# Moving a kernel's main SBUF pool down by 128 bytes: weight buffers and operand tiles at another distance

## The chip, the cores and the metric

The kernel runs on one core of a Trainium2 chip. TensorE (PE) multiplies matrices into PSUM; VectorE (DVE) and ScalarE (ACT) do elementwise work; GpSimd (POOL) and SyncE (SP) here mostly issue DMAs. The metric is the device time of one execution in microseconds (us). Before the change three runs took 2003.82, 2023.43 and 2035.96 us; the median is 2023.43 us.

SBUF addresses in this document are byte addresses within a partition, as the built program has them. All 128 partitions use the same address for a tile.

## The reference, cut to what matters

One decoder layer on 512 tokens of width 2048, all in float32:

```python
mod = (c_act @ w_ada[l] + b_ada[l]).reshape(B, N_MOD, D)        # 2048 x 12288
h = rmsnorm(x, g_norm_mix[l]) * (1.0 + sc1) + sh1
proj = jnp.einsum('bsd,de->bse', h, w_in[l])                    # 2048 x 5120
o_attn = stick_breaking_attention(...)                          # 8 heads of 128
hr = rg_lru(causal_depthwise_conv(xr, ...), ...)                # width 1024
mixed = concat([rmsnorm(o_attn, ...), rmsnorm(hr * gelu(xg), ...)])
x = x + gt1 * einsum('bse,ed->bsd', mixed, w_out[l])            # 2048 x 2048
h = rmsnorm(x, g_norm_mlp[l]) * (1.0 + sc2) + sh2
hid = square(relu(einsum('bsd,df->bsf', h, w_mlp_in[l])))       # 2048 x 8192
x = x + gt2 * einsum('bsf,fd->bsd', hid, w_mlp_out[l])          # 8192 x 2048
return rmsnorm(x, g_norm_final)
```

## The kernel before, in words

**Matmuls.** Each float32 factor is split into a rounded high part and the low remainder, and every product is three matmuls: high by high, high by low, low by high (`mm3`, L258; the same three written out at L470 to L472 and at L1099 to L1101). A matmul has a stationary operand of 128 columns, brought in by its own weight load (PEld in the profile), and a moving operand that streams past it. While one matmul streams, the weight load of the next one runs.

**Stages.** Up to about 660 us the projections of `w_in`, the attention heads, the recurrence and the first three quarters of `w_out` are worked out, mostly with moving operands of 512 columns. From there on the moving operands are 256 columns wide (half of the tokens): the last quarter of `w_out` and the first block of the MLP (`half_product`, L988), then the other 15 blocks of the MLP's first matrix and its second matrix by a Strassen-like scheme with seven products in place of eight (`strassen`, L1080). Each step of that scheme loads one block of 1024 weight columns, forms four sums of its quarters on DVE (L1057, L1064, L1065), splits quarters and sums into high and low parts (`operands`, L1050), and issues 7 products x 2 halves x 3 = 42 matmuls. The last stretch is a normal product and the output.

**Buffers.** Moving operands of the MLP are `a` tiles, 64 buffers of 2,048 bytes. Three quarters of a weight block, split, lie in `w3` buffers (3,072 bytes, called small here); the four sums, split, lie in buffers of 4,096 bytes (called large), which `T` takes in turn from the tags `w4` four times and `w5` once (L82, L98). Of the seven products of a step, the four with t1 to t4 read large buffers and the other three read `w3` (`PRODUCTS`, L1075).

**Where they lie.** The main pool `sp` begins low in SBUF with constants, then `ga` (16 bytes a buffer, laid out at a pitch of 32), then `pad` (L140, `PAD` floats that nothing uses), then `cb`, `n` and `a`. On top of it, on the left side, stands one of two pools that follow each other in time: `front` (`wr`, `wh`, `wl`) and `mlp`, which begins with `shift` (`SHIFT` = 16 floats that nothing uses), then `w5` and `w3`. The right side hangs from the top of SBUF and doesn't depend on the main pool: `x` and `tt` first, later `ts`, `raw` and `w4`. In the built program before the change:

| tiles | address of the first | remainder by 512 |
|---|---|---|
| `cb`, `n`, `a` | 19,904, 28,096, 38,336 | 448 |
| `wr`, `wh`, `wl` | 169,408, 177,600, 183,744 | 448 |
| `w5`, `w3` | 169,472, 173,568 | 0 |
| `x`, `tt`, `ts`, `raw`, `w4` | 192,000, 208,384, 192,000, 200,192, 212,480 | 0 |

Every buffer of a tag has the same remainder, and every slice that a matmul takes of one begins a multiple of 512 bytes into it. So a weight load of the MLP begins 64 bytes behind the moving operand, modulo 512, for large and small buffers alike; with `wh` and `a` in the earlier stages the distance is 0.

**What sets the order.** A scheduler orders each engine's instructions by data dependence and by priorities that the kernel gives (`tc.high_priority`). `ga` holds the partial sums of a DVE operation (L211, L1200) until a second DVE operation adds them up (L220, L1206).

Of the kernel before, what the change touches and what calls it, by code (L numbers as in the profile page):

```python
# [40 lines left out]

URGENT = 150
EVAC = 88
PAD, SHIFT = 24, 16

BUFS = {"cb": 2, "a": 64, "ga": 4, "n": 5}
COLS = {
    "wr": 512, "wh": 512, "wl": 512, "x": 1024, "cb": 1024, "tt": 1280, "n": 512, "a": 512, "ga": 4,  # L50
    "raw": 1024, "ts": 1024, "w3": 768, "w4": 1024, "w5": 1024, "shift": SHIFT,
# [13 lines left out]
def hybrid_layer_kernel(  # L65
# [35 lines left out]
    def new(tag, dt=F32, cols=None):  # L101
        count[0] += 1
        pool, bufs = (sp, BUFS[tag]) if tag in BUFS else pools[tag][:2]
        return pool.tile([P, cols or COLS[tag]], dt, tag=tag, name=f"{tag}_{count[0]}", bufs=bufs)
# [1355 lines left out]
```

## Time and profile before

| what | value |
|---|---|
| runs before | 2003.82, 2023.43, 2035.96 us |
| the profiled execution's own time | 2022.22 us |
| its span, first to last instruction | 2020.5 us |
| mean granted TensorE clock | 0.995 |
| matmuls | 14,532 |
| PE busy | 1967.8 us (97%) |
| DVE busy | 1761.0 us (87%) |
| ACT busy | 1076.0 us (53%) |

The views give busy time of an engine, the number of instructions (x), and the mean duration of one. Matmuls overlap, so their durations add up to more than the time; how often one starts is read from a count in a stretch of time. An instruction counts in a stretch if any part of it lies there, so a stretch in which matmuls of duration d follow each other without a gap holds (stretch + d) / (time from start to start) of them.

### The profile page before, as it was taken

To read this page: it belongs to the slowest core of one execution; us is meant where nothing else is said; L and a number is where in the kernel's file an instruction comes from. 1 tells how busy PE (TensorE), PEld (TensorE's weight loads), DVE (VectorE), ACT (ScalarE), POOL (GpSimd) and SP (SyncE) were. 2 spreads that over 40 slices of the span, in tenths; PEclk is the share of its full clock that TensorE was granted. 3 is DMA by queue.
4 is the path that set the end of the run, shared out by engine and by line. 5 is a ranking of instruction groups with operands and counts; after the bars stand their busy time and mean duration, and the time that the engine had idled before them with its cause. 6 is when DMAs were issued, how large, how long until landed. Compare 5 with 4: busy or idle time off the path is not lost. (4 is left out here: it accounts for less than half of the span.)

```text
span 2020.5 us, 37927 instructions
## 1 busy us (share of the span) xinstructions
PE 1967.8 (97%) x14532; PEld 1857.3 (92%) x14532; DVE 1761.0 (87%) x2971; ACT 1076.0 (53%) x1572; POOL 181.1 (9%) x283
## 2 busy tenths in 40 slices
PE   8999999999999998999999999999999999999997
PEld 6789898788888998999999999999999999999996
DVE  8998776878998599999999999999778778778986
ACT  5443564786433385555555555456445555555542
POOL 0000000000000000112112112200011110210000
PEclk9999999999999999999999999999999999999998
DMA  9896655546779544666666657665486667667744
GB/s 363 301 319 211 211 158 179 182 151 217 229 251 360 171 137 150 216 202 218 204 196 228 209 178 230 222 205 179 142 300 224 222 243 250 234 243 256 241 152 152
DMA packets 205624, 441.45 MB, mean 218 GB/s; under 512 B 20353, under 2 KB 41985, under 8 KB 205442
## 3 DMA queue, kind: packets, MB, share of 16 engines
q1 hardware_dynamic: 178642, 360.78, 54.1%
q0 software_dynamic: 21760, 71.32, 9.5%
q10 hardware_dynamic: 5040, 6.93, 1.0%
q8 instruction: 114, 1.87, 0.4%
q14 instruction: 68, 0.56, 0.1%
HBM read 375.25 MB, written 63.70 MB: 217 GB/s over the span
## 5 line engine op out<-in xcount | busy, mean ns | idle before, releaser
L1101 PE MATMUL ps_mm<-a,w 128*128 128x256 f32 x1696 | 472.4, 279 | 1.6 <-DVE w L122 1.6
L1099 PE MATMUL ps_mm<-a,w 128*128 128x256 f32 x1696 | 472.0, 279 | 1.9 <-DVE a L1111 1.1
L1100 PE MATMUL ps_mm<-a,w 128*128 128x256 f32 x1696 | 472.3, 279 | 0.2 <-DVE a L122 0.2
L1069 ACT ACTIVATE w<-ts 128x1024 fp32r<-128x1024 f32 x244 | 258.4, 1059 | 249.4 <-DVE ts L1065 224.8
L1101 PE MATMUL ps_z<-a,w 128*128 128x256 f32 x1304 | 364.8, 280 | 7.5 <-DVE w L122 7.5
L1099 PE MATMUL ps_z<-a,w 128*128 128x256 f32 x1304 | 364.6, 280 | 3.1 <-ACT a L1110 1.5
L122 DVE TENSOR_TENSOR w<-ts,w 128x1024 fp32r<-128x1024 f32 x244 | 297.5, 1219 | 79.0 <-PE ps_mm L1100 44.6
L1100 PE MATMUL ps_z<-a,w 128*128 128x256 f32 x1304 | 364.0, 279 | 0.1
L1099 PEld LDWEIGHTS ps_mm<-a,w 128*128 128x128 f32 x1696 | 321.5, 190 | 2.5 <-issue 2.0
L1101 PEld LDWEIGHTS ps_mm<-a,w 128*128 128x128 f32 x1696 | 318.8, 188 | 2.1 <-DVE w L122 2.0
L1100 PEld LDWEIGHTS ps_mm<-a,w 128*128 128x128 f32 x1696 | 318.6, 188 | 0.6 <-DVE a L122 0.6
L1063 ACT ACTIVATE w<-raw 128x768 fp32r<-128x768 f32 x244 | 204.6, 839 | 211.9 <-PE ps_mm L1100 101.0
L122 DVE TENSOR_TENSOR w<-raw,w 128x768 fp32r<-128x768 f32 (+1 forms) x296 | 267.0, 903 | 35.7 <-ACT w L244 22.7
L1101 PEld LDWEIGHTS ps_z<-a,w 128*128 128x128 f32 x1304 | 246.0, 189 | 9.2 <-DVE w L122 9.1
L1099 PEld LDWEIGHTS ps_z<-a,w 128*128 128x128 f32 x1304 | 248.0, 190 | 4.5 <-ACT a L1110 1.7
L1100 PEld LDWEIGHTS ps_z<-a,w 128*128 128x128 f32 x1304 | 245.7, 188 | 0.6 <-DVE a L122 0.6
L244 ACT ACTIVATE wh<-wr 128x512 fp32r<-128x512 f32 (+1 forms) x184 | 113.1, 618 | 150.9 <-PE ps_mm L262 67.6
L259 PE MATMUL ps_mm<-a,wh 128*128 128x512 f32 x448 | 176.5, 394 | 4.0 <-DVE a L460 1.7
L263 PE MATMUL ps_mm<-a,wl 128*128 128x512 f32 x448 | 175.5, 392 | 1.0 <-DVE wl L122 0.7
L1057 DVE TENSOR_TENSOR ts<-raw 128x512 f32<-128x512 f32 x244 | 166.4, 683 | 10.2 <-DMA raw<-in_w_mlp_out_dram 9.7
L262 PE MATMUL ps_mm<-a,wh 128*128 128x512 f32 x448 | 174.7, 390 | 0.0
L211 DVE SCALAR_TENSOR_TENSOR x<-x,cb 128x1024 f32<-128x1024 f32 x108 | 131.1, 1217 | 29.5 <-DMA x<-in_w_adaT_dram 29.3
(332 smaller groups left out, 4137.9 us busy)
## 6 DMA issues: line engine op xcount, KB each, us to landing
raw<-in_w_mlp_out_dram SPq DMA_DIRECT2D x124, 512.0 KB, 4.1
raw<-in_w_mlp_in_dram SPq DMA_DIRECT2D x120, 512.0 KB, 3.8
x<-in_w_adaT_dram SPq DMA_DIRECT2D x108, 512.0 KB, 5.9
wr<-in_w_in_dram SPq DMA_DIRECT2D x160, 256.0 KB, 3.5
tt<-in_w_adaT_dram SPq DMA_DIRECT2D x52, 512.0 KB, 6.8
part<-a POOLq DMA_DIRECT2D x84, 256.0 KB, 3.8
a<-part SPq DMA_DIRECT2D x84, 256.0 KB, 6.4
prod<-a POOLq DMA_DIRECT2D x63, 256.0 KB, 5.9
```

What stands on the lines that cost most here:

```text
L122: tt(out=out, in0=full, in1=f32(high), op=ALU.subtract)
L211: ins = stt(out=t, in0=t, scalar=1.0, in1=cb[q_], op0=ALU.mult, op1=ALU.mult, accum_out=self.ga[:, q_ : q_ + 1],)
L244: act(h[:, :n], r[:, :n], AF.Copy)
L259: first = mm(out, wh, ah, start=start, stop=False, **kw)
L262: mm(out, wh, al, start=False, stop=False, **kw)
L263: mm(out, wl, ah, start=False, stop=stop, **kw)
L1057: tt(out=t[:, : 2 * HT].rearrange("p (a b) -> p a b", a=2), in0=r[:, HT : 3 * HT].rearrange("p (a b) -> p a b", a=2), in1=r[:, q_(0)].unsq ...
L1063: act(h, r[:, HT:], AF.Copy)
L1069: act(h, t, AF.Copy)
L1099: mm(out, wh[:, blk(i)], ah, start=st, stop=False, **kw)
L1100: mm(out, wh[:, blk(i)], al, start=False, stop=False, **kw)
L1101: mm(out, wl[:, blk(i)], ah, start=False, stop=j == js[-1], **kw)
```

## The change

Two numbers change. `ga` has 2 buffers in place of 4, and the unused `pad` behind it 8 floats in place of 24. Both are laid out ahead of `cb`, `n` and `a`, so everything of the main pool from `cb` on, and the left pools on top of it, begins 2 x 32 + 16 x 4 = 128 bytes lower. The right side stays.

```diff
-PAD, SHIFT = 24, 16
+PAD, SHIFT = 8, 16
...
-BUFS = {"cb": 2, "a": 64, "ga": 4, "n": 5}
+BUFS = {"cb": 2, "a": 64, "ga": 2, "n": 5}
```

In the built program after the change `cb`, `n`, `a`, `wr`, `wh` and `wl` have the remainder 320, `w5` and `w3` 384, and `x`, `tt`, `ts`, `raw` and `w4` still 0. So the weights in `w4` (and those that `half_product` keeps in `ts`) begin 192 bytes behind the moving operand, modulo 512, and those in `w3` and `w5` still 64.

Every engine has the same instructions in the same order as before. What differs beside addresses is a few waits of DVE for its own earlier instructions, since a `ga` buffer comes round again sooner. The following rows are from DVE's order in the attention heads; `x` is a row of `w_ada`, `cb` the conditioning vector, and a name in brackets is the counter that an instruction waits for.

```order
 L122 TENSOR_TENSOR wl_4707<-wr_4704,wh_4706 128x512 [waits DMAHW4_49,PE_49,Activation_49]
 L211 SCALAR_TENSOR_TENSOR x_4725,ga_4722<-x_4725,cb_82 128x1024 [waits DMAHW0_49]
-L211 SCALAR_TENSOR_TENSOR x_4813,ga_4812<-x_4813,cb_81 128x1024 [waits DMAHW2_49]
+L211 SCALAR_TENSOR_TENSOR x_4813,ga_4812<-x_4813,cb_81 128x1024 [waits DMAHW2_49,DVE_49]
 L639 SCALAR_TENSOR_TENSOR tt_4608<-ps_z_4593,tt_4608 128x512 [waits Activation_49]
 L122 TENSOR_TENSOR wl_4733<-wr_4730,wh_4732 128x512 [waits DMAHW5_49,PE_49,Activation_49]
-L639 SCALAR_TENSOR_TENSOR tt_4608<-ps_z_4594,tt_4608 128x512 [waits DVE_49]
+L639 SCALAR_TENSOR_TENSOR tt_4608<-ps_z_4594,tt_4608 128x512
```

Nothing has moved here; the second L211 row has gained a wait for DVE's own counter, and a later row has lost one.

## The prediction

> **What bounds the kernel now.** I read the page's first part, then the stretches of time by engine, and then the same stretches for PE alone.
>
> ```profile
> span 2020.5 us, 37927 instructions
> PE 1967.8 (97%) x14532; PEld 1857.3 (92%) x14532; DVE 1761.0 (87%) x2971; ACT 1076.0 (53%) x1572; POOL 181.1 (9%) x283
> ```
>
> PE is the bound: it lacks only 52.7 us of the span. But a busy PE only says that some matmul is under way, not how fast they follow each other. So the stages are next (columns: the stretch, busy time and count of each engine, granted clock, DMA share, GB/s).
>
> ```profile
> 0.00:660.00 660.00, 640.11 (x3248) 541.92 (x3249) 556.52 (x970) 345.12 (x541) 18.00 (x19) 1.00 0.72 241
> 660.00:800.00 140.00, 131.76 (x1043) 126.87 (x1041) 112.14 (x225) 86.22 (x168) 7.40 (x13) 0.98 0.45 138
> 800.00:1400.00 600.00, 592.99 (x5140) 589.16 (x5141) 588.51 (x1005) 333.07 (x445) 95.39 (x141) 1.00 0.64 209
> 1400.00:1900.00 500.00, 499.69 (x4248) 499.49 (x4247) 406.65 (x601) 261.62 (x343) 59.18 (x110) 1.00 0.67 237
> 1900.00:2020.50 120.50, 103.26 (x859) 99.91 (x858) 97.14 (x175) 49.98 (x77) 1.09 (x2) 0.96 0.48 157
> ```
>
> From 800 to 1900 us PE has no gap to speak of (592.99 of 600, 499.69 of 500). In the first of these stages DVE is as full as PE (588.51 of 600), in the second it has room (406.65 of 500). The granted clock is 1.00 in both. Yet 5,140 matmuls in 600 us and 4,248 in 500 us are not the same rate, though the shapes are the same. The view by stretches for PE alone, and the mean duration in each, show why.
>
> ```profile
> 301.00:310.00 9.00, 9.00 (x78) 1.00 0.39 114
> 500.00:550.00 50.00, 50.00 (x222) 1.00 0.72 231
> 674.00:700.00 26.00, 26.00 (x223) 1.00 0.50 157
> 806.00:819.00 13.00, 13.00 (x112) 1.00 0.68 237
> 828.00:898.00 70.00, 70.00 (x597) 1.00 0.70 224
> 921.00:935.00 14.00, 14.00 (x121) 1.00 0.48 147
> 942.00:1162.00 220.00, 220.00 (x1944) 1.00 0.66 213
> 1361.00:1375.00 14.00, 12.86 (x108) 1.00 0.73 254
> 1402.00:1882.00 480.00, 480.00 (x4078) 1.00 0.68 239
> ```
>
> Groups of matmuls in four of these, in the same order (count, busy us, mean ns of one):
>
> ```profile
> L471 PE MATMUL ps_mm<-wh,a 128*128 128x256 f32 x26 | 7.4, 283 | 0.0
> ...
> L1099 PE MATMUL ps_mm<-a,w 128*128 128x256 f32 x88 | 24.7, 281 | 0.0
> ...
> L1101 PE MATMUL ps_mm<-a,w 128*128 128x256 f32 x337 | 93.0, 276 | 0.0
> ...
> L1101 PE MATMUL ps_mm<-a,w 128*128 128x256 f32 x690 | 193.9, 281 | 0.0
> ```
>
> From 942 to 1162 us a matmul starts every (220 + 0.276) / 1944 = 113.3 ns; from 1402 to 1882 us every (480 + 0.281) / 4078 = 117.8 ns. Both hold to the end of the stretch, at the same granted clock, with the same shapes and all weights 64 bytes behind the moving operand. So there is a **short spacing** (113.3 ns, duration 276) and a **long spacing** (117.8 ns, duration 281), 4.5 ns apart. At 301 us, in the value projection, whose stationary `a` and moving `wh` lie at distance 0, a matmul of the same size starts every (9 + 0.283) / 78 = 119.0 ns, give or take one count: slower still. The weight loads follow:
>
> ```profile
> L1099 PEld LDWEIGHTS ps_mm<-a,w 128*128 128x128 f32 x688 | 132.1, 192 | 0.0
> L1100 PEld LDWEIGHTS ps_mm<-a,w 128*128 128x128 f32 x689 | 129.3, 188 | 0.0
> ...
> L1099 PEld LDWEIGHTS ps_mm<-a,w 128*128 128x128 f32 x336 | 63.1, 188 | 0.0
> ...
> L472 PEld LDWEIGHTS ps_mm<-wl,a 128*128 128x128 f32 x26 | 5.0, 192 | 0.0
> L471 PEld LDWEIGHTS ps_mm<-wh,a 128*128 128x128 f32 x26 | 5.0, 192 | 0.0
> L470 PEld LDWEIGHTS ps_mm<-wh,a 128*128 128x128 f32 x25 | 4.8, 192 | 0.0
> ```
>
> At the long spacing one load in three takes 192 ns and not 188 (first two rows); at the short one none does (third); at distance 0 all three kinds do (last three). I read this as the weight load getting into the way of the matmul that streams beside it, and the distance between the two addresses as one thing that decides it. It can't be the only one, since both spacings occur at 64.
>
> **The change part by part.**
>
> *Addresses of the MLP's weights.* The strassen loop ran 244 times (the first DVE row below), so it issued 244 x 42 = 10,248 matmuls. Of seven products four read large buffers, of which four in five are `w4`: 16 in 35, or 4,685 matmuls, go from 64 to 192. The other 5,563 stay at 64. The half products add some 900 of both kinds, in about the same shares.
>
> What the long spacing costs now: the six rows above that have it (674, 806, 828, 921, 1361 and 1402 us) hold 5,239 matmuls, so 5,239 x 4.46 ns = 23.4 us. If all of it went, the execution would take 2022.2 - 23.4 = 1998.8 us. If the rest of the MLP (some 11,160 matmuls less 5,239) fell into the long spacing, it would take 2022.2 + 5,921 x 0.00446 = 2048.6 us. The three runs (2003.82 to 2035.96) lie inside these two ends: how much of each run has the long spacing explains their spread of 32 us, though no view shows it for the runs that weren't profiled.
>
> No row of the trace has a weight load 192 bytes behind its moving operand. The nearest are 64 (113.3 or 117.8) and 0 (119.0; but 227.0 for 512 columns in the row at 500 us, that is (50 + 0.389) / 222, or 113.5 for 256: no cost, with a weight load half as often). So a large buffer at 192 is bounded by 113.3 below and 119.0 above, and I see no reason for less than 113.3: no stretch shows it. I take 113.3, as further from 0 is the direction in which the rows get better. That takes 16/35 of the 23.4 us, or 10.7 us. The small buffers stay at 64, where both spacings can hold; but the long one holds now in stretches in which every load has the same distance, and after the change the distance jumps by 128 bytes several times in each step of 42. I take it that half of their 12.7 us goes too: 6.3 us. Sum: 2022.2 - 10.7 - 6.3 = **2005 us** (1999 to 2012 by all or none of the second term). In the stage from 800 to 1400 us DVE has only 11.5 us free, so what PE gains there (the stretches at 806, 828, 921 and 1361, 111 us and so 4 us of the 23.4) may come back as waits; that is inside the range.
>
> By the Trainium skill (TensorE: Matmul & The Clock Gate, on what each phase of a matmul is for) PE has two independent read ports, and loading the next weights takes no bandwidth from the running matmul. By that rule no distance matters and the sum is 2022. The rows at 301 and 942 us speak against it as a full account: the same shape, the same clock, 119.0 against 113.3 ns.
>
> *Addresses on DVE and ACT.* Some operand pairs lie at another distance too (`raw` and `w3`, `x` and `cb`). Before, they lie at 0 or 64:
>
> ```profile
> L122 DVE TENSOR_TENSOR w<-ts,w 128x1024 fp32r<-128x1024 f32 x244 | 297.5, 1219 | 79.0 <-PE ps_mm L1100 44.6 <-PE ps_z L1100 21.3 <-PE ps_o L1100 7.1
> L122 DVE TENSOR_TENSOR wl<-wr,wh 128x512 fp32r<-128x512 f32 x176 | 120.0, 685 | 29.6 <-ACT wh L244 29.1
> L122 DVE TENSOR_TENSOR w<-raw,w 128x512 fp32r<-128x512 f32 x52 | 35.3, 687 | 23.0 <-ACT w L244 22.7
> L122 DVE TENSOR_TENSOR x<-a,x 128x512 fp32r<-128x512 f32 x8 | 5.3, 680 | 0.0
> ```
>
> The last three rows are one operation of one size at distances 0, 0 and 64: 685, 687, 680 ns. I take no cost. The bound is 1% of the w3 splits and sums, some 3 us on either side, and it would count only in the DVE-full stage.
>
> *The earlier stages.* `wr`, `wh`, `wl` and `a` move together; their distances stay. Nothing.
>
> *The waits on `ga`.* Three L211 rows gain a wait for DVE's own counter. DVE issues in order, and the reader waited for (L220, below) stands ahead of them anyway. Queued behind are the splits of `w_in` blocks, for which PE waits. At most a reader's duration each, under 1 us together; I take 0.
>
> ```profile
> L220 DVE SCALAR_TENSOR_TENSOR mods<-ga,vec 128x1 f32<-128x1 f32 x80 | 20.8, 260 | 1.2
> ```
>
> The profiled execution took 2022.22 us, 1.7 over its span, and lies 1.2 under the median of the runs.
>
> **The rivals.**
>
> *The distance doesn't decide.* Which spacing holds is drawn anew whenever PE stalls, and the address has no part in it at 64 or beyond. For: both spacings occur at 64, and 480 us of the long one run without a break. Against: the row at distance 0, where the slower rate holds throughout. Then the runs scatter as before, 2004 to 2036, with the middle near **2022**. This is also where the skill's rule on separate ports would leave it.
>
> *192 is a bad distance.* The loads from large buffers conflict as at distance 0, at 119.0 ns, always. Place: the four t products of each step and the half products that use `w4`. With 4,685 + some 500 matmuls at 5.7 ns more than the short spacing that is 29.6 us, in place of the 10.7 that they lose now: 2022.2 + 18.9 = **2041**, and if the small ones get the long spacing as well (5,900 x 4.46 = 26.3 in place of 12.7) 2055. It is slower than before from the point at which the large buffers average more than 113.3 + 10.7/5,185, that is 115.4 ns. For: nothing shows what repeats with 512 bytes, so 192 may be as near to a collision as 0. Against: 64, nearer to 0, is already free for 220 us on end.
>
> *The change doesn't move what it says, or hits something else.* The built program has the addresses as stated. What is left is a DVE or DMA effect of the new remainders (320 in place of 448), up or down: a few us by the bounds above, but unknown in kind.
>
> **How the numbers follow.** Forecast 45%, no influence 25%, bad distance 24%, something else 6%, half of it up and half down. The prediction is 2005. The range takes in the forecast (1999 to 2012), nearly all of the second case, and the lower half of the third: 1997 to 2046. About 2% is what a measurement of this kernel can tell from no change: below 1983 or above 2064. Below 1983 would need a matmul rate that no stretch shows: 3%. Above 2064 would need the bad distance for large and a rate worse than any row's for small buffers: 5%. Within 2%: 92%.
>
> **What would show it.** In the profile after, stretches of the second MLP stage with over 4,150 matmuls in 480 us (against 4,078) and durations of 276 would show the short spacing; weight loads of 188 ns for all three lines likewise. If large and small buffers differ, durations of matmuls will lie between 276 and 283 with a mixture inside each step. The forecast is wrong if a stretch without stalls still shows 281 and 117.8 ns for hundreds of us (then distance doesn't decide), or 283 and 119 (then 192 is bad). DVE rows should keep 1219, 949 and 685 ns; if they change by more than 1%, the second term of the sum is wrong.

## The result and the profile after

After the change the median is **2004.92 us** (20 runs, 2001.96 to 2009.35); the kernel before, run beside it, took 2016.14 us (20 runs, 2003.82 to 2035.96). The ratio is 0.9944, with a 95% interval from 0.9922 to 0.9965: a gain of 0.6% that the interval separates from nothing, and far under 2%. The range of the runs shrank from 32 to 7.4 us. The shortest execution before lies inside the range after; what went are the long ones. The prediction counted from the one profiled execution before, 2022.22 us; against the median beside it the gain is 11.2 us.

The profiled execution after took 2004.49 us, 17.7 us less than the one before. The first part of its page:

```profile
span 2002.8 us, 37929 instructions
PE 1947.9 (97%) x14532; PEld 1837.3 (92%) x14532; DVE 1761.3 (88%) x2971; ACT 1076.5 (54%) x1572; POOL 181.2 (9%) x283
```

PE has the same matmuls and 19.9 us less of busy time; the time in which it is idle is 54.9 us, 2.2 more than before. The stretches by engine, with the same borders as in the prediction (columns: the stretch, busy time and count of PE, PEld, DVE, ACT and POOL, granted clock, DMA share, GB/s):

```profile
0.00:660.00 660.00, 641.33 (x3261) 544.38 (x3262) 558.63 (x972) 346.56 (x542) 17.58 (x19) 1.00 0.72 242
660.00:800.00 140.00, 131.42 (x1060) 127.06 (x1059) 114.52 (x229) 86.90 (x167) 8.40 (x14) 0.99 0.47 141
800.00:1400.00 600.00, 591.30 (x5122) 585.82 (x5122) 586.25 (x999) 332.85 (x444) 94.91 (x139) 1.00 0.64 207
1400.00:1900.00 500.00, 497.37 (x4378) 496.45 (x4378) 422.51 (x629) 269.44 (x356) 60.28 (x111) 1.00 0.69 244
1900.00:2002.80 102.80, 86.50 (x720) 83.64 (x718) 79.38 (x146) 40.74 (x65) 0.00 (x0) 0.95 0.45 149
```

The count of matmuls tells where the time came from. From 1400 to 1900 us PE got through 4,378 in place of 4,248. These 130 are worth 130 x 0.1133 = 14.7 us, most of the 17.7. From 800 to 1400 us, where DVE has little room (586 of 600 us), it got through 18 **fewer** (5,122 for 5,140). The first two stretches gave 13 and 17 more.

PE alone in two long stretches in which it is never idle, and then matmuls and weight loads by group in the second of them (count, busy us, mean ns of one, idle):

```profile
942.00:1088.00 146.00, 146.00 (x1289) 1.00 0.67 215
1402.00:1856.00 454.00, 454.00 (x4008) 1.00 0.70 247
```

```profile
L1101 PE MATMUL ps_mm<-a,w 128*128 128x256 f32 x674 | 186.0, 276 | 0.0
```

```profile
L1099 PEld LDWEIGHTS ps_mm<-a,w 128*128 128x128 f32 x675 | 126.7, 188 | 0.0
L1100 PEld LDWEIGHTS ps_mm<-a,w 128*128 128x128 f32 x674 | 126.5, 188 | 0.0
L1101 PEld LDWEIGHTS ps_mm<-a,w 128*128 128x128 f32 x674 | 126.5, 188 | 0.0
```

From 1402 to 1856 us a matmul starts every 454.276 / 4,008 = 113.3 ns, at the duration 276 of the short spacing, where before the long spacing held for 480 us. Intervals beside loads from large and from small buffers have the same mean there, 113.3 ns.

For the rest I laid the trace's matmuls beside the built program's, one by one, so that the distance of each weight load from the operand that streams past at that moment is known. The 11,208 intervals from one start to the next in the MLP sort like this (excess is what they are above 113.3 ns; up to 115 ns is called short below, 115 to 119.5 long):

| kernel | up to 115 ns | 115 to 119.5 | 119.5 to 124 | longer (stalls) | excess at 115 to 119.5, us | excess in stalls, us |
|---|---|---|---|---|---|---|
| before | 5,467 | 5,572 | 37 | 132 | 24.7 | 34.7 |
| after | 10,378 | 599 | 69 | 162 | 2.6 | 41.5 |

So 22.1 us of the long spacing went, and 6.8 us came back in stalls, 15.3 us together. One stretch weighs most: between 1400 and 1900 us the excess of the long spacing was 18.4 us before and is 0.1 after. Most of the other 2.4 us up to 17.7 are stalls of the 512-column matmuls of the earlier stages (21.8 us before, 19.9 after), whose distances the change leaves alone.

### The profile page after: what moved, and what is told of

Read it like the earlier page. It is cut to its first block, busy times and chain, and to the rows that moved or that the text cites. A ratio compares the mean times of both kernels' runs of the same rounds, so it can differ in the third digit from the quotient of the medians.

```text
span 2002.8 us, 37929 instructions
## 1 busy us (share of the span) xinstructions
PE 1947.9 (97%) x14532; PEld 1837.3 (92%) x14532; DVE 1761.3 (88%) x2971; ACT 1076.5 (54%) x1572; POOL 181.2 (9%) x283
## 3 DMA queue, kind: packets, MB, share of 16 engines
q1 hardware_dynamic: 178642, 360.78, 54.9%
## 5 line engine op out<-in xcount | busy, mean ns | idle before, releaser
L122 DVE TENSOR_TENSOR w<-ts,w 128x1024 fp32r<-128x1024 f32 x244 | 298.6, 1224 | 58.6 <-PE ps_mm L1101 26.5
L122 DVE TENSOR_TENSOR wl<-wr,wh 128x512 fp32r<-128x512 f32 (+1 forms) x184 | 124.7, 681 | 33.3 <-ACT wh L244 32.5
```

The lines of the kernel that those rows point to most:

```text
L122: tt(out=out, in0=full, in1=f32(high), op=ALU.subtract)
```

## The experiments

None of these kernels changes what is computed, only where buffers lie, or, in the last, the order of products. Distances are those of the MLP's weight loads behind the moving operand modulo 512, large buffers / small buffers; before is 64/64, after 192/64. Ratios are against the kernel before, run beside them on the same chip; its median there was 2026.59, 2023.46 and 2015.53 us for the first four, the next four and the last four kernels, so ratios of different groups aren't compared with each other. The kernel after did not run again beside these, so a difference of a few us from its 2004.92 is not read; the traces carry the argument.

**1. The place without the distance (64/64).** The main pool stays where the change puts it, `ga` has 2 buffers, and the right side goes down by 128 bytes too. The added line moves all numbers behind it up by one.

```diff
+    top.tile([P, 32], F32, tag="down", name="down")
```

> The change as it is, but with an unused tile of 128 bytes at the top of SBUF, which moves ts, raw, w4 (and x, tt) down by the same 128 bytes: weights in large and small buffers lie 64 bytes behind the moving operand again, while ga keeps its 2 buffers and the main pool its new place. If the distance decides (64 can have both spacings), the runs scatter as before the change, between 2004 and 2036 us with a median near 2016, and long stretches of 117.8 ns can come back. If the place of the main pool or the smaller ga made the gain, the runs stay at 2002 to 2009 us and the spacing at 113.3 ns.

Measured: median 2025.53 us (12 runs, 2018.49 to 2032.49), ratio 1.0015 [0.9984, 1.0045]. PE from 1410 to 1890 us, and a group of matmuls there:

```profile
1410.00:1890.00 480.00, 480.00 (x4078) 1.00 0.68 239
```

```profile
L1102 PE MATMUL ps_mm<-a,w 128*128 128x256 f32 x690 | 193.9, 281 | 0.0
```

The long spacing is back, with the very count of before (4,078), and over all 9,002 of the 11,208 intervals are between 115 and 119.5 ns. So `ga` and the main pool's place alone bring nothing. With the distances as before, the long spacing is as before. Nor is it the address of one operand by itself: before and in experiments 2, 3 and the first of 8, all weight buffers of the MLP have the same addresses and only the `a` tiles move; after and in experiments 1, 2, 7 and the first of 5, the `a` tiles have one address and only weights move.

**2. All at 192.** From the kernel after, `w5` and `w3` go up by 128 bytes:

```diff
-PAD, SHIFT = 8, 16
+PAD, SHIFT = 8, 48
```

> The change with SHIFT 48 in place of 16: small buffers lie 192 bytes behind the moving operand too, so all weights of the MLP have one distance and nothing jumps between products. If 192 is a distance without the long spacing, the runs are as narrow as after the change, 2000 to 2008 us, and the MLP's matmuls stay at 113.3 ns. If it was the jump between two distances that broke the long spacing, long stretches of 117.8 ns come back and the runs scatter over 2004 to 2036 us.

Measured: median 2029.89 us (12 runs, 2023.29 to 2032.61), ratio 1.0034 [1.0003, 1.0064]. PE from 1405 to 1910 us, with groups of matmuls and of weight loads:

```profile
1405.00:1910.00 505.00, 504.67 (x4283) 1.00 0.67 237
```

```profile
L1101 PE MATMUL ps_mm<-a,w 128*128 128x256 f32 x718 | 201.0, 280 | 0.0
```

```profile
L1100 PEld LDWEIGHTS ps_mm<-a,w 128*128 128x128 f32 x719 | 135.1, 188 | 0.0
L1101 PEld LDWEIGHTS ps_mm<-a,w 128*128 128x128 f32 x719 | 135.0, 188 | 0.0
L1099 PEld LDWEIGHTS ps_mm<-a,w 128*128 128x128 f32 x719 | 134.5, 187 | 0.0
```

A matmul starts every 505.28 / 4,283 = 118.0 ns, a few stalls included: the long spacing. It holds for 10,871 of the 11,208 intervals, more than at 64 alone. **So 192 isn't a free distance**, though in the kernel after the large buffers at 192 run at 113.3 ns. Nor are the weight loads longer: 188 ns, as at the short spacing. My reading of the 192 ns as the mark of a load that is in the way is wrong: at 64 one load in three has them at the long spacing and none at the short, at 0 all have them, and at 192 none does even at the long spacing.

**3. All at 0.** From the kernel after:

```diff
-PAD, SHIFT = 8, 16
+PAD, SHIFT = 40, 0
...
-BUFS = {"cb": 2, "a": 64, "ga": 2, "n": 5}
+BUFS = {"cb": 2, "a": 64, "ga": 4, "n": 5}
```

> ga 4, PAD 40, SHIFT 0: operands and all weight buffers have the remainder 0, distance 0 in the MLP as in the value projection. If distance 0 is bad there as here, some 11,160 matmuls go to 119 or 120 ns: 1999 + 11,160 x 6.5 ns = 2071 us, with a spread of a few us, durations of 283 and weight loads of 192 ns. If the distance does nothing, 2004 to 2036 us as before.

Measured: median 2050.49 us (6 runs, 2047.53 to 2055.54), ratio 1.0145 [1.0095, 1.0196]. PE from 831 to 1396 us, and a group there:

```profile
831.00:1396.00 565.00, 565.00 (x4708) 1.00 0.62 204
```

```profile
L1099 PE MATMUL ps_mm<-a,w 128*128 128x256 f32 x775 | 219.4, 283 | 0.0
```

565.283 / 4,708 = 120.1 ns without a break. The third rate of the value projection holds in the MLP too, and the short spacing came up in 12 intervals only. Distance does decide, at 0. The time is 20 us under the 2071 expected, though the excess of the intervals up to 124 ns, 74 us, is as expected: the stalls, which the expectation left as they were, fell from 34.7 to 17.7 us. A slower PE waits less for the others.

**4. The earlier stages at 192.** From the kernel after, a gap of 192 bytes ahead of `wr`, `wh` and `wl`:

```diff
-    "front": ("left", {"wr": 4, "wh": 3, "wl": 3}),
+    "front": ("left", {"gap": 1, "wr": 4, "wh": 3, "wl": 3}),
```

> The change with 192 unused bytes ahead of wr, wh and wl: in the earlier stages the w_in weights no longer lie at distance 0 from the a tiles but at 192 (in the value projection, whose stationary operand is the a tile, at minus 192). If distance 0 causes the 120 ns of the value projection, its 768 matmuls go to 113.3 ns and the kernel gains 768 x 6.7 = 5 us: 2000 us against 2005. The 512-column matmuls (227 ns) should stay. If the value projection is slower for another reason (its stationary operand), nothing changes.

Measured: median 2003.60 us (12 runs, 1999.38 to 2008.96), ratio 0.9912 [0.9883, 0.9941]. That isn't told apart from the kernel after (2001.96 to 2009.35). The value projection between 290 and 330 us, and PE in the two stretches that the prediction used:

```profile
L472 PE MATMUL ps_mm<-wl,a 128*128 128x256 f32 x57 | 15.8, 277 | 0.0
L471 PE MATMUL ps_mm<-wh,a 128*128 128x256 f32 x57 | 15.7, 276 | 0.0
...
301.00:310.00 9.00, 9.00 (x82) 1.00 0.43 116
500.00:550.00 50.00, 50.00 (x220) 1.00 0.72 228
```

The projection's durations fell from 283 to 276 and 277 (279 in the third line), and in the 9 us stand 82 matmuls in place of 78. Over its 768 matmuls the mean without stalls fell from 119.8 to 115.8 ns, not to 113.3. But the 512-column matmuls got no better: 220 in 50 us in place of 222, (50 + 0.39) / 220 = 229 ns for 227. What little the projection gains (2.3 us in all) is given back there: 1,728 matmuls, 229.6 ns for 227.4 on average without stalls.

**5. 192 with 128, 128 with 64, 64 with 0.** Three mixtures with other steps between the two distances; the first starts from the kernel after, the others from the kernel before.

```diff
-PAD, SHIFT = 8, 16
+PAD, SHIFT = 8, 32
```

> The change with SHIFT 32: large buffers 192 bytes behind the moving operand, small ones 128, so the distance jumps by 64 bytes between products and not by 128. Theory of the jump (any change of distance in mid-stream gives the long spacing a chance to end, and the short one survives it): 2002 to 2012 us, the MLP mostly at 113.3 ns. Theory that 64 must be one of the two distances, because it alone can hold the short spacing: near 2025 to 2033 us, as with 192 throughout.

```diff
-PAD, SHIFT = 24, 16
+PAD, SHIFT = 8, 16
```

> ga 4, PAD 8, SHIFT 16: large buffers at 128, small ones at 64, again a jump of 64 bytes, with 64 in it. Theory of the jump: 2002 to 2012 us, mostly 113.3 ns. If the jump has to be 128 bytes: 2004 to 2036 us with long stretches of 117.8 ns.

```diff
-PAD, SHIFT = 24, 16
+PAD, SHIFT = 24, 0
```

> The kernel before with SHIFT 0: large buffers stay at 64, small ones go to 0, the distance at which every matmul took 120 ns when all weights had it. If each load pays for its own distance, some 5,900 matmuls take 120 ns and the rest 113.3 or 117.8: 1999 + 5,900 x 6.7 ns = 2038 us, up to 2062. If the jump of 64 bytes matters and the distance itself does not, the spacing is 113.3 ns for small buffers too: 2002 to 2012 us.

Measured: 2036.74 us (10 runs, 2033.83 to 2041.13), ratio 1.0084 [1.0051, 1.0117]; 2022.52 us (10 runs, 2018.71 to 2023.60), ratio 1.0013 [0.9973, 1.0054]; 2039.99 us (10 runs, 2037.99 to 2043.44), ratio 1.0091 [1.0054, 1.0129]. PE from 942 to 1162 us, one row of each in this order:

```profile
942.00:1162.00 220.00, 220.00 (x1864) 1.00 0.64 207
...
942.00:1162.00 220.00, 220.00 (x1891) 1.00 0.65 211
...
942.00:1162.00 220.00, 220.00 (x1855) 1.00 0.64 207
```

The kernel before had 1,944 there. Sorted by distance over the whole MLP, means without stalls: 192 and 128 ran at 117.8 and 118.5 ns; 128 and 64 at 118.0 and 115.3, with 60% of the intervals at 64 short, at most 34 in a row; 64 and 0 at the long spacing (97% between 117 and 119.5) and at 120 (77%). None of the three came to the 2002 to 2012 us of the jump theory, and the first (2036.74) is slower than the other theory had it too (2025 to 2033). So a mixture as such, or one whose distance steps by 64, is not what helped.

**6. The earlier stages with 64 and 192 mixed.** From the kernel after, `wh` at 64 and `wl` at 192:

```diff
-    "front": ("left", {"wr": 4, "wh": 3, "wl": 3}),
+    "front": ("left", {"gap": 1, "wr": 4, "wh": 3, "gap2": 1, "wl": 3}),
```

> The change with 64 unused bytes ahead of wr and wh and 128 more ahead of wl, so that in the earlier stages wh and wl lie at 64 and 192 from the a tiles. In the value projection the distance then jumps inside every group of three matmuls. Theory of the jump: its 768 matmuls go from 120 to 113.3 ns, 5 us less than the change: 2000 us. If a jump there does nothing: some 117.8 ns, as with one distance of 192 there, and 2003 us.

Measured: median 2005.69 us (10 runs, 2001.78 to 2008.77), ratio 0.9942 [0.9905, 0.998]; again not told apart from the kernel after. PE in the same two stretches as in experiment 4:

```profile
301.00:310.00 9.00, 9.00 (x78) 1.00 0.39 109
500.00:550.00 50.00, 50.00 (x217) 1.00 0.70 223
```

The 512-column matmuls are slower still (50.39 / 217 = 232 ns), and the value projection isn't at the short spacing. In these stages the mixture did not do what it does in the MLP; the order of high and low parts is another there, and I didn't follow it further.

**7. Nearly all at 192: only the one `w5` buffer at 64.** From the kernel after, a gap of 128 bytes between `w5` and `w3`:

```diff
-    "mlp": ("left", {"shift": 1, "w5": 1, "w3": 6}),
+    "mlp": ("left", {"shift": 1, "w5": 1, "gap": 1, "w3": 6}),
```

> All weights 192 bytes behind the moving operand (alone: 2030 us, the long spacing nearly throughout), but for the one buffer w5, which stays at 64 (an unused 128 bytes stand behind it). w5 is every fifth large buffer, so a change of the distance from 192 to 64 and back comes in about two of five steps only, and over nine in ten weight loads keep 192. If a change from 192 to 64 in mid-stream ends the long spacing, it ends within a few steps (some 10 to 20 us) after each stall: 2003 to 2012 us, the MLP mostly at 113.3 ns. If each load pays for its own distance, 2025 to 2031 us.

Measured: median 2004.70 us (9 runs, 2001.62 to 2007.95), ratio 0.9932 [0.9909, 0.9955]. PE from 942 to 1163 us, and a group there:

```profile
942.00:1163.00 221.00, 221.00 (x1953) 1.00 0.66 214
```

```profile
L1101 PE MATMUL ps_mm<-a,w 128*128 128x256 f32 x340 | 93.8, 276 | 0.0
```

This is the run that decides. 9,900 loads lie at 192 and 1,308 at 64, yet nearly the whole gain is there: 221.276 / 1,953 = 113.3 ns, and 83% of the loads at 192 run at the short spacing, where with all at 192 there were 2%. The same loads at the same distance are free or not by what comes between them. That points to the passage from one distance to the other.

The traces show the passages themselves. Starts of matmuls in the kernel after, behind a stall (start, duration, in us); the weight loads lie at 192 up to the one that runs beside the matmul at 1243.71 and at 64 from the one beside 1243.83 on, with the next passage to 192 at 1244.53:

```profile
1243.36 0.28 PE L1100 MATMUL ps_z<-a,w 128*128 128x256 f32 x1
1243.47 0.28 PE L1101 MATMUL ps_z<-a,w 128*128 128x256 f32 x1
1243.59 0.28 PE L1099 MATMUL ps_z<-a,w 128*128 128x256 f32 x1
1243.71 0.28 PE L1100 MATMUL ps_z<-a,w 128*128 128x256 f32 x1
1243.83 0.28 PE L1101 MATMUL ps_z<-a,w 128*128 128x256 f32 x1
...
1244.30 0.28 PE L1099 MATMUL ps_mm<-a,w 128*128 128x256 f32 x1
1244.41 0.28 PE L1100 MATMUL ps_mm<-a,w 128*128 128x256 f32 x1
1244.53 0.28 PE L1101 MATMUL ps_mm<-a,w 128*128 128x256 f32 x1
1244.64 0.28 PE L1099 MATMUL ps_mm<-a,w 128*128 128x256 f32 x1
1244.75 0.28 PE L1100 MATMUL ps_mm<-a,w 128*128 128x256 f32 x1
```

From 1243.36 to 1243.83 four intervals take 0.47 us, 118 ns each. The next four, unrounded 115, 116, 123 and 118 ns, are a transition. From 1244.30 to 1244.75 four take 0.45 us, 113 ns each, and it stays so through the passage back to 192. Over whole traces, I count the places at which four intervals in a row are long and either the next one is the first beside a load at the other distance (64 or 192), or no passage is near. Short behind it means that, after four more intervals, three in a row are short. Places without a passage overlap, so one change of spacing counts at several:

| kernel | passages met at the long spacing | of them short behind it | places without a passage | of them short behind |
|---|---|---|---|---|
| after | 41 | 21 (51%) | 171 | 0 |
| experiment 7 | 71 | 19 (27%) | 1,035 | 6 (0.6%) |
| experiment 9 | 58 | 25 (43%) | 434 | 0 |
| before (all 64) | none | | 5,420 | 7 (0.1%) |
| experiment 1 (all 64) | none | | 8,861 | 10 (0.1%) |
| experiment 2 (all 192) | none | | 10,737 | 22 (0.2%) |

Of the passages from 192 to 64 met at the long spacing 56 of 128 were short behind, of those from 64 to 192 only 9 of 42. The short spacing, once there, survives passages: in the kernel after 1,136 of the 1,166 passages from 192 to 64 that met it left it as it was. In the three kernels with one distance 66 of the 70 changes between four long and four short intervals, either way, have a stall between them; in the kernel after 18 of the 27 changes from long to short have none, but a passage. So a stall can bring up the long spacing. Without passages it then stayed for up to 4,092, 3,664 and 4,101 intervals in a row (before, experiments 1 and 2), 430 to 480 us; with them for at most 47, 96 and 70 (after, experiments 7 and 9).

**8. Two further distances: all at 128, and 256 with 128.** Both edits are from the kernel after:

```diff
-PAD, SHIFT = 8, 16
+PAD, SHIFT = 8, 32
...
-BUFS = {"cb": 2, "a": 64, "ga": 2, "n": 5}
+BUFS = {"cb": 2, "a": 64, "ga": 4, "n": 5}
```

> ga 4, PAD 8, SHIFT 32: all weights 128 bytes behind the moving operand. If what counts repeats every 128 bytes, 128 is like 0: 120 ns throughout, durations of 283, about 2050 us. If it repeats every 512 and 128 is an ordinary distance, 117.8 ns with or without short stretches: 2015 to 2033 us.

```diff
-PAD, SHIFT = 8, 16
+PAD, SHIFT = 0, 32
...
-BUFS = {"cb": 2, "a": 64, "ga": 2, "n": 5}
+BUFS = {"cb": 2, "a": 64, "ga": 1, "n": 5}
```

> ga 1, PAD 0, SHIFT 32: large buffers at 256, small ones and w5 at 128, a change of 128 bytes as in the change under study, but neither at 64 nor at 192 (with one ga buffer a few instructions of the first stages stand in another order, so the MLP's spacing is what counts here). If a change of 128 bytes in mid-stream is all it takes: 113.3 ns in the MLP and 2002 to 2012 us. If both distances are of the bad kind (multiples of 128, like 0): 120 ns and 2040 to 2052 us.

Measured: 2040.44 us (4 runs, 2038.10 to 2042.44), ratio 1.0122 [1.0083, 1.0161]; 2044.59 us (4 runs, 2041.75 to 2047.70), ratio 1.0144 [1.0111, 1.0178]. In the second a few instructions of the earlier stages change places, since one `ga` buffer is not enough there. PE from 942 to 1162 us, in this order:

```profile
942.00:1162.00 220.00, 220.00 (x1857) 1.00 0.64 207
...
942.00:1162.00 220.00, 220.00 (x1845) 1.00 0.62 207
```

With all at 128 the mean without stalls is 118.7 ns, spread from 115 to 123 rather than at one value; in the second kernel the loads at 256 have 120.0 and those at 128 again 118.7. In neither do two intervals in a row stay at 114 ns or less. The second kernel's distance steps by 128 as often as in the kernel after, and nothing is freed. So the step alone doesn't do it either: of the distances tried, the multiples of 128 (0, 128, 256) have no lasting short spacing, 64 alone has it at times (1,338 intervals in a row before), 192 alone hardly (63), and 64 and 192 together have it for most of the MLP (4,049 in a row in the kernel after).

**9. Fewer passages.** From the kernel after, the seven products of a step are issued so that those with large buffers stand together: two changes of distance in a step in place of six. That holds for the three steps in five whose large buffers are all `w4`. In the other two `w5` holds the high or the low part, so the distance also changes inside products, some 16 times in a step with either order. In all, passages fell from 2,493 to 1,923 only.

```diff
-            for b, (an, wn) in zip(bs, PRODUCTS):
+            for x in (0, 2, 1, 3, 4, 6, 5):
+                b, (an, wn) = bs[x], PRODUCTS[x]
```

> The change with the products of a step issued in another order (first, third, second, fourth, fifth, seventh, sixth), so that the matmuls on small and on large buffers stand together and the distance changes twice in a step and not six times. If changes of the distance end the long spacing, it lasts about three times as long after each stall: the matmuls at 117 to 119 ns go from some 600 to 1200 to 2000, 3 to 6 us more than the change, 2006 to 2012 us. If they have nothing to do with it, the number stays near 600 and the time near 2005 us.

Measured: median 2018.52 us (10 runs, 2014.74 to 2023.53), ratio 1.0015 [0.9987, 1.0043]. The intervals at 115 to 119.5 ns rose from 599 to 1,050. The expectation had 1200 to 2000, but for a third of the passages, and they fell by a quarter. In experiment 7, with 1,600 passages, they are 1,614: the fewer passages, the more long intervals. But here that is only 2.0 us (2.6 to 4.6). The larger part of the loss of 13.6 us against the kernel after is something else: stalls, 50.2 us in place of 41.5. PE's longest waits for `combine`, which adds up the block before, from 800 to 2003 us, this kernel first and the kernel after second (the added line moves the numbers by one, so its L1112, L1116 and L1118 are L1111, L1115 and L1117 there; columns: total us, times, longest):

```profile
PE ps_mm L1100 <- DVE a L1116: 3.6, 4, 1.3
PE ps_z L1100 <- DVE a L1118: 3.3, 2, 1.9
PE ps_z L1100 <- DVE a L1112: 2.4, 3, 1.1
PE ps_z L1100 <- DVE a L1116: 2.1, 2, 1.3
```

```profile
PE ps_z L1099 <- DVE a L1115: 1.6, 3, 0.5
PE ps_z L1099 <- ACT a L1110: 1.5, 1, 1.5
PE ps_mm L1099 <- DVE a L1111: 1.2, 1, 1.2
```

`combine` empties the accumulators in the order of the old issue. With the new order PE asks for accumulators that it hasn't emptied yet; that this makes up the whole loss isn't shown. This run therefore speaks for the passages only by its count, not by its time.

## Why the prediction was right, and where it wasn't

The time was right (2005 predicted, 2004.92 measured) and so was the frame: PE bound, two spacings, the long one costing some 23 us, the earlier stages unchanged. But the two terms of the sum were put together from one wrong reason and one that was far too small.

*The first term (10.7 us: large buffers at 192 are free, "further from 0 is the direction in which the rows get better").* The amount came in, the reason falls. All at 192 is the long spacing in 97% of the intervals, while in the kernel after 90% of those beside loads at 192 are short. The rows were 0 and 64 only, and a line through two points was taken for a direction. What frees loads at 192 in the kernel after is the small buffers at 64 between them.

*The second term (6.3 us: the jump of the distance ends half of the long spacing of the small buffers).* This is the mechanism that the experiments bear out, for large buffers as well, and the term was mis-sized: not half of 12.7 us but 22.1 of the whole 24.7 us (the prediction had 23.4 from six stretches).

*What was left out.* The sentence that gains in the DVE-full stage may come back as waits was right, and no term of the sum stood for it: stalls cost 6.8 us more. (In experiments 4 and 6, with the same MLP addresses, stalls are 38.6 and 38.4 us against 34.7 before, some 4 us more.) From 800 to 1400 us the long spacing's excess fell by 3.6 us and stalls rose by 5.8 us, so the gain is gone altogether (18 matmuls fewer). Experiments 4 and 7 put 5,148 and 5,144 matmuls there, so even those are level with before. I read DVE, busy 586 to 589 of 600 us, as what sets the rate there while the spacing is short. PE's spacing still counts: in experiment 1, with the long one through most of that stage, PE got through 5,063. Here are the two rows of experiments 4 and 7 (same columns as above):

```profile
800.00:1400.00 600.00, 591.41 (x5148) 586.52 (x5147) 589.25 (x1003) 334.53 (x447) 96.37 (x141) 1.00 0.65 209
...
800.00:1400.00 600.00, 591.94 (x5144) 587.96 (x5143) 588.79 (x1004) 334.76 (x446) 94.81 (x139) 1.00 0.64 208
```

With the second mechanism at its true size and no stalls the sum would have been 2022.2 - 22.1 = 2000, some 4 us under the profiled 2004.49. Halving one term stood in for the loss that had no term, so the agreement of the total is partly luck.

*DVE's addresses (no cost).* Right within about 1%:

```profile
L122 DVE TENSOR_TENSOR w<-ts,w 128x1024 fp32r<-128x1024 f32 x244 | 298.6, 1224 | 58.6 <-PE ps_mm L1101 26.5 <-PE ps_z L1101 15.0 <-ACT w L1069 6.5
L122 DVE TENSOR_TENSOR w<-raw,w 128x768 fp32r<-128x768 f32 x244 | 233.0, 955 | 15.3 <-ACT w L1063 15.3
L122 DVE TENSOR_TENSOR wl<-wr,wh 128x512 fp32r<-128x512 f32 x176 | 121.4, 692 | 30.4 <-ACT wh L244 29.5 <-issue 0.2
```

1224, 955 and 692 ns for 1219, 949 and 685. The last rose by 1% though its operands keep their distance, and in experiment 2, with `a`, `wr`, `wh` and `wl` at the same addresses as in the kernel after, it is 684: the differences go with the execution, not with the addresses. The waits for `ga` appear in no view.

*The rivals.* "Distance doesn't decide" falls with experiment 3 and with experiment 1 against the kernel after, but half of it is true: at the one distance of 64 which spacing holds changes at stalls. I take that draw to be the spread of 32 us; two traces agree with it (before: 5,572 long intervals, 2022.22 us; experiment 1: 9,002, 2032.49 us), the other runs were not profiled. "192 is a bad distance" is true in experiment 2 for 192 alone, at 118.0 ns and not at 119 or 120, and it is false beside 64. "The change hits something else" wasn't seen.

*What would show it.* Over 4,150 matmuls in 480 us was the mark; 4,008 in 454 us are 4,237 in 480. The sign "weight loads of 188 ns" is worth nothing, as experiment 2 showed.

*The rule on separate ports.* By the Trainium skill (TensorE: Matmul & The Clock Gate, on what each phase of a matmul is for) a load of the next weights takes no bandwidth from the running matmul. Experiment 3 against the kernel after speaks against that as the whole account: only addresses differ in the MLP, and the rate is 120.1 against 113.3 ns at a granted clock of 1.00 in both.

**What stays open.** Why the multiples of 128 bytes behave alike, why a passage between 64 and 192 frees the short spacing (and one between 256 and 128 doesn't), and what at a stall decides for one spacing or the other. The runs show that these things happen, not by which part of the memory or of PE. It also stays open whether a mixture of 64 with an odd multiple of 64 other than 192 does the same, and why the mixture failed in the earlier stages.

## What to carry to other kernels

When PE is 97% busy, count its matmuls in stretches without stalls and divide: a mean duration hides that the same matmul at the same clock can run at 113.3, 117.8 or 120.0 ns, and a spread between runs of one kernel can come from which of them holds for how long. Where the address of the next weights against that of the streaming operand can be chosen, it can be tried with unused bytes alone; here multiples of 128 were the worst, one distance throughout was a draw or worse, and 64 and 192 in turn were best. A row at two distances is no trend: test the distance alone (all buffers at 192) before crediting it.

## What was not expected of the hardware

- Three rates of one matmul of 256 columns at the granted clock of 1.00: 113.3, 117.8 and 120.0 ns, each held for thousands of matmuls (4,008, 4,078 and 4,708 in the stretches shown).
- A memory in PE's pace: a spacing once there holds for up to 480 us and thousands of equal matmuls, and it changes nearly always at stalls or at passages between distances. All at 192 had 222 short intervals of 11,208, and nearly the same addresses with one buffer moved by 128 bytes had 9,385.
- A weight load of 192 ns in place of 188 is no mark of a slow pace: at 192 bytes all loads take 188 ns at the long spacing too. At 64 one in three takes 192 ns at the long spacing and none at the short; at 0 all do.
- Distance 0, the worst for 256 columns at 120.0 ns, is the best of those tried for matmuls of 512 columns: 227 ns, against 229 and 232 ns on average in the two kernels that moved them.
